# RWKV part of a hybrid layer: the distances between dependent steps set one by one, bank evictions grouped, and the mLSTM output gates computed there and passed through memory

## The chip, the cores and the metric

One core of one Trainium2 chip. The metric is the device time of one execution in microseconds (us); lower is better. TensorE is called PE here, VectorE DVE, ScalarE ACT, GpSimd POOL, and SyncE, which issues most of the loads, SP.

## The reference

One layer of a hybrid decoder on 256 positions of 2048 channels, all in float32. One wide projection `h @ w_in` feeds three mixers (a Mamba-2 scan called SSD, an RWKV-7 recurrence, an mLSTM) and three sigmoid branch gates; an output projection, a residual with LayerNorm and a gated MLP follow. Cut to what the change touches:

```python
proj = h @ w_in
(ssd_z, ssd_xbc, ssd_dt, rwkv_p, ml_qk, ml_v, ml_o, ml_i, ml_f, gate_pre) = split(proj)
# rwkv7_mixer(rwkv_p, ...), 32 heads of 64
p = p + (token_shift(p) - p) * mu
r, k, v, w_lo, a_lo, g_lo = split(p)
decay, a, g = exp(-exp(log_w)), sigmoid(a0 + a_lo @ a2), sigmoid(g_lo) @ g2
y = rwkv7_recurrence(r, decay, kh, v, -kk, kk * a)    # S_t = S_{t-1} diag(w) + (S_{t-1} a) b^T + v k^T; y = S r
y = head_layer_norm(y) * ln_w + ln_b
y = (y + sum(r * kh * r_k) * v) * g
# mlstm_mixer: 8 heads of 256 value channels
y_mlstm = sigmoid(ml_o) * (group_rms_norm(mlstm_chunked(q, k, v, ...)) * norm_w)
g_ssd, g_rwkv, g_mlstm = split(sigmoid(gate_pre))
merged = g_ssd * (y_ssd @ proj_ssd) + g_rwkv * (y_rwkv @ proj_rwkv) + g_mlstm * (y_mlstm @ proj_mlstm)
x = layer_norm(alpha * x + merged @ w_out)            # and then the gated MLP
```

## The kernel before, in words

**Weights.** Every float32 product is made of three matmuls on halves of the operands (high x high, high x low, low x high). A weight arrives in chunks of 2 x 128 rows by 512 columns: SP issues the load into `wraw` (four buffers), ACT casts the high half `whi`, DVE subtracts to get the low half `wlo` (three buffers of each), and PE multiplies. Cast and subtraction together are called a cut. One 128-row step of a projection of 512 columns is a *unit*; 16 units make a projection. In the form of r, k and v a unit is 12 matmuls of 256 columns (lines L250 to L254; output channels on partitions); in the form of the gates it is 6 matmuls of 512 columns (L272 to L274; positions on partitions). Accumulators lie in `acc` (four PSUM banks); the mixers' own matmuls use `mix` (two banks) and `seq` (two banks).

**The RWKV part** (`rwkv`) is ordered by hand on PE, DVE, ACT and POOL: in this stretch each of these engines runs its instructions in the order in which the program writes them. Two generators are interleaved. `weights()` walks the list `order` of projections: v of group 0, then for groups 1 to 3 k, v, r, one RWKV branch gate (`(1, g - 1)`) and one entry of `later` (SSD and mLSTM branch gates), and then what is left: 22 projections, 352 units. `groups()` walks the four groups of 8 heads, and a `yield n` in it says that n weight units go in before its next step. So the numbers behind `yield` are the distances, in units of PE work, between a step and the one that needs its result. If a step is not ready after that distance, PE waits.

The steps of one group, in order:
- `pre`: decay, `kh`, the normalised k.
- `pairs`: for each of four chunks, products of operands (`l1e`, `l1o`, `bk`; POOL and DVE make them), 8 matmuls into two banks (L730), four masked evictions by DVE into `bp` and into the other half of `l1e`/`l1o` (L733, L734), and transposes of `bk` with an ACT copy (L740).
- `inverse`: the triangular inverse, a chain of 31 pairs of operations on POOL (L770, L772: `si`, `yi`); beside it transposes of v and the per-head sums from `sqh` and `sql`; then a shuffle and two transposes on DVE (L791 to L795: `yi`, `x`, `xt`), and two rounds of small matmuls (L806 and after).
- `recurrence`: four chunks of dependent matmuls and evictions (`zve`, `zvo`, L853 to L867).
- `output_gate`: `gx`, `gw` by POOL, then matmuls (L896).
- `tail`: mean, squares, variance, square root, reciprocal and product on `yt` (L909 to L922), transposes of `yt` on PE (L929), an ACT activation into `yo` (L933), and two DVE products.

`weave` merges two such generators: `inverse(g)` with `tail(g - 1)`, and `recurrence(g)` with `pre(g + 1)` and `output_gate(g)`. The tail of group g thus runs while the inverse of group g+1 is under way.

In `rkv_units`, a finished projection is evicted by `lerp` (four times: an ACT activation, then a DVE part, L372 and L373), but only once the step named in `after` has been written: v of group g after `tail(g - 2)`, r after `pairs(g - 1)`, k after `kh` of g - 1. Until then the generator yields `False`: the unit is counted, and holds no matmul.

`gate_units` makes one branch gate: 16 units, a sigmoid into page `p18`, and a write to `gdram` (issued from ACT). Later `branch` reads it back.

**The rest** (SSD, branch projections, mLSTM, output projection, MLP) is ordered by a scheduler that works from the dependences. In `ml_in`, the mLSTM makes for each pair of heads a value projection, an output-gate projection (`block_tm(W, C_MO + 512 * j, ...)` and a sigmoid into `so`) and two heads (`ml_head`: scores L1076, nine value matmuls L1088, normalisation on DVE and ACT, transposes L1141, and `yml` L1148).

## Time and profile before

| | before |
|---|---|
| runs | 2484.13, 2489.2 and 2953.28 us; median 2489.2 us |
| profiled execution | 2489.84 us, span 2488.1 us |
| mean granted TensorE clock | 0.981 |
| busy | PE 2381.0 us (96%), DVE 1550.7 (62%), ACT 1244.6 (50%), POOL 447.1 (18%) |
| moved from and to memory | 443.46 MB, 178 GB/s over the span |

The profiled execution is one run under the hardware profiler; its span is what the trace covers. A "granted clock" is the share of full speed that TensorE was given. PE's busy time counts its matmuls; DVE, ACT and POOL are busy while an instruction runs. A row of waits such as "PE seq L929 <- DVE yt L922" reads: PE stood idle before an instruction of line 929 that writes `seq`, until DVE's instruction of line 922 on `yt` was done.

### The profile page before, as it was taken

How to read it: one execution, taken by the hardware profiler on the slowest of the kernel's cores; microseconds unless marked ns; L12 is line 12 of the kernel's file. 1: busy time of each engine (PE TensorE's matmuls, PEld its weight loads, DVE VectorE, ACT ScalarE, POOL GpSimd, SP SyncE). 2: the span in 40 equal slices, each digit the busy share in tenths (PEclk: the TensorE clock that was granted, in tenths of full speed). 3: DMA queues.
4: the chain of work that ended last, by engine and by line, in shares of the span. 5: the costliest groups of instructions: out<-in, count | busy, mean ns of one | idle time of the engine just before them, and what ended most of it. 6: DMA issues, size and time to landing. Idle time of an engine off the chain costs nothing.

```text
span 2488.1 us, 41458 instructions
## 1 busy us (share of the span) xinstructions
PE 2381.0 (96%) x16602; PEld 2136.5 (86%) x16602; DVE 1550.7 (62%) x1888; ACT 1244.6 (50%) x1625; POOL 447.1 (18%) x480
## 2 busy tenths in 40 slices
PE   7999989988989999999999999999999999999997
PEld 7888787787777899988899888787999999997886
DVE  6685675664664668775556666556766666664545
ACT  4635545555455546653445666444554554454333
POOL 0026333351361104330100001310300000000000
PEclk9999999999999999999999999999999999999999
DMA  8545445444455666656666667655655656557664
GB/s 236 148 138 155 126 121 155 129 138 134 145 177 164 217 178 183 191 187 231 216 188 178 183 175 219 219 188 189 183 184 182 186 179 187 184 167 231 193 196 149
DMA packets 282578, 443.46 MB, mean 178 GB/s; under 512 B 25688, under 2 KB 118288, under 8 KB 282000
## 3 DMA queue, kind: packets, MB, share of 16 engines
q1 hardware_dynamic: 279792, 431.89, 57.0%
q10 hardware_dynamic: 2016, 6.82, 0.7%
q8 instruction: 130, 2.13, 0.3%
q0 software_dynamic: 576, 2.10, 0.2%
q14 instruction: 64, 0.52, 0.1%
HBM read 428.10 MB, written 12.62 MB: 177 GB/s over the span
## 4 chain that ended last, share of the span: by engine, by line
PE 78%; POOL 5%; DVE 5%; issue 4%; ACT 4%; DMA 3%; SPq 0%; ACTq 0%; DVEq 0%; POOLq 0%
PE acc L250 13%; PE acc L254 13%; PE acc L252 13%; PE acc L272 12%; PE acc L273 11%; PE acc L274 11%; POOL yi L772 2%; POOL si L770 2%; ACT whi L157 1%; DVE wlo L158 1%; PE mix L730 1%; DVE wlo L234 1%; DMA wraw<-in_ffn_w_down 1%; PE mix L617 1%; DMA wraw<-in_proj_mlstm 1%
## 5 line engine op out<-in xcount | busy, mean ns | idle before, releaser
L234 DVE TENSOR_TENSOR wlo<-wraw,whi 128x1024 fp32r<-128x1024 f32 (+2 forms) x580 | 742.7, 1282 | 559.0 <-ACT whi L233 553.2
L233 ACT CAST whi<-wraw 128x1024 fp32r<-128x1024 f32 (+2 forms) x580 | 603.2, 1041 | 705.1 <-PE acc L274 333.2
L250 PE MATMUL acc<-xh,whi 128*128 128x256 f32 x3104 | 886.9, 286 | 6.2 <-ACT whi L233 3.8
L254 PE MATMUL acc<-xh,wlo 128*128 128x256 f32 x3104 | 882.4, 285 | 8.8 <-DVE wlo L158 6.1
L252 PE MATMUL acc<-xl,whi 128*128 128x256 f32 x3104 | 881.8, 284 | 0.0
L250 PEld LDWEIGHTS acc<-xh,whi 128*128 128x128 f32 x3104 | 598.5, 193 | 11.6 <-ACT whi L233 4.6
L254 PEld LDWEIGHTS acc<-xh,wlo 128*128 128x128 f32 x3104 | 597.9, 193 | 12.2 <-DVE wlo L158 7.6
L252 PEld LDWEIGHTS acc<-xl,whi 128*128 128x128 f32 x3104 | 598.8, 193 | 0.9 <-issue 0.7
L158 DVE TENSOR_TENSOR wlo<-wraw,whi 128x1024 fp32r<-128x1024 f32 x176 | 226.4, 1297 | 218.2 <-ACT whi L157 217.5
L272 PE MATMUL acc<-whi,xh 128*128 128x512 f32 x640 | 257.8, 415 | 5.8 <-ACT whi L157 5.8
L273 PE MATMUL acc<-wlo,xh 128*128 128x512 f32 x640 | 257.2, 402 | 4.4 <-DVE wlo L158 4.4
L274 PE MATMUL acc<-whi,xl 128*128 128x512 f32 x640 | 255.4, 399 | 0.0
L157 ACT CAST whi<-wraw 128x1024 fp32r<-128x1024 f32 x176 | 181.9, 1047 | 131.1 <-PE acc L252 74.7
L272 PEld LDWEIGHTS acc<-whi,xh 128*128 128x128 f32 x640 | 123.4, 193 | 35.7 <-ACT whi L157 6.7
L273 PEld LDWEIGHTS acc<-wlo,xh 128*128 128x128 f32 x640 | 123.7, 193 | 29.0 <-DVE wlo L158 6.6
L274 PEld LDWEIGHTS acc<-whi,xl 128*128 128x128 f32 x640 | 123.4, 193 | 26.1
L273 PE MATMUL acc<-wlo,ah 128*128 128x512 f32 x322 | 125.5, 390 | 0.7 <-DVE wlo L234 0.7
L274 PE MATMUL acc<-whi,al 128*128 128x512 f32 x322 | 125.3, 389 | 0.0
L272 PE MATMUL acc<-whi,ah 128*128 128x512 f32 x322 | 112.1, 389 | 0.8 <-ACT whi L233 0.8
L770 POOL TENSOR_TENSOR si<-yi,ni 128x126 f32<-128x126 f32 (+22 forms) x124 | 76.4, 616 | 183.6 <-DVE ni L757 174.2
L1219 POOL TENSOR_TENSOR fc<-fc 128x512 f32<-128x512 f32 (+1 forms) x22 | 27.9, 1270 | 449.7 <-DVE fc L381 444.9
L381 DVE SCALAR_TENSOR_TENSOR fc<-acc,fcols,fc 128x255 f32<-128x255 f32 (+1 forms) x172 | 77.0, 477 | 14.0 <-ACT fc L378 12.5
(357 smaller groups left out, 2993.9 us busy)
## 6 DMA issues: line engine op xcount, KB each, us to landing
wraw<-in_w_in SPq DMA_DIRECT2D x368, 512.0 KB, 3.7
wraw<-in_ffn_w_up SPq DMA_DIRECT2D x336, 256.0 KB, 3.1
wraw<-in_ffn_w_down SPq DMA_DIRECT2D x84, 512.0 KB, 4.4
wraw<-in_proj_rwkv SPq DMA_DIRECT2D x32, 512.0 KB, 4.4
wraw<-in_proj_ssd SPq DMA_DIRECT2D x32, 512.0 KB, 4.5
wraw<-in_proj_mlstm SPq DMA_DIRECT2D x32, 512.0 KB, 5.1
wraw<-in_w_out SPq DMA_DIRECT2D x32, 512.0 KB, 4.0
gdram<-gate ACTq DMA_DIRECT2D x12, 512.0 KB, 3.6
```

Source lines behind the costliest of these rows:

```text
L157: nc.scalar.copy(out=hi, in_=self.raw[i])
L158: nc.vector.tensor_tensor(out=lo, in0=self.raw[i], in1=hi.bitcast(F32), op=ALU.subtract)
L233: nc.scalar.copy(out=hi[:, :n, :width], in_=r)
L234: nc.vector.tensor_tensor(out=lo[:, :n, :width], in0=r, in1=hi[:, :n, :width].bitcast(F32), op=ALU.subtract)
L250: nc.tensor.matmul(a, lhsT=wh[:, o:o + m], rhs=X.h(kt), start=st, stop=False, skip_group_check=True)
L252: nc.tensor.matmul(a, lhsT=wh[:, o:o + m], rhs=X.l(kt), start=False, stop=False, skip_group_check=True)
L254: nc.tensor.matmul(a, lhsT=wl[:, o:o + m], rhs=X.h(kt), start=False, stop=kt == nkt - 1, skip_group_check=True)
L272: nc.tensor.matmul(acc[tt], lhsT=X.h(kt)[:, s], rhs=wh, start=kt == 0, stop=False)
L273: nc.tensor.matmul(acc[tt], lhsT=X.h(kt)[:, s], rhs=wl, start=False, stop=False)
L274: nc.tensor.matmul(acc[tt], lhsT=X.l(kt)[:, s], rhs=wh, start=False, stop=kt == nkt - 1)
L381: nc.vector.scalar_tensor_tensor(out=dst[:, j:], in0=ps[:, :T - j], scalar=v(wname, (width - 1 - j) * nch + ct), in1=dst[:, j:], op0=ALU.m ...
L770: gps.tensor_tensor(out=tv, in0=Yo[:, j:j + 1, :e].to_broadcast(sh), in1=N[:, j + 1:32, j:j + 1].to_broadcast(sh), op=ALU.mult)
```

## The change

Six edits, all in or around the RWKV part:

1. **Distances.** The numbers behind `yield` in `inverse`, `recurrence`, `output_gate` and `tail` are set anew, step by step, most of them higher; in `inverse` the pair of cast and subtraction for `sqh` and `sql` is taken apart with one unit between.
2. **Evictions of r, k and v.** All four ACT activations come first, then a `yield False`, then the four DVE parts.
3. **Pairs.** Half of the masked evictions (those into `l1e` and `l1o`) become a plain ACT copy; the mask is multiplied in three units later by POOL.
4. **Tail.** Both pairs of transposes of a bank are written before the two activations that evict it.
5. **Output gates of the mLSTM.** They join `later` as four more projections of the RWKV part (26 projections, 416 units) and go to `gdram`, whose first axis grows from 3 to 4. `ml_in` no longer computes them; it reads `so` back by a DMA on SP.
6. With that, two entries of `later` follow each group's gate instead of one.

```diff
...
 COL = {"r": C_R, "k": C_K, "v": C_V}
+def gate_column(i, j):
+    return 512 * j + (C_GATE + 2048 * i if i < 3 else C_MO)
...
         for j in range(4):
-            self.lerp(cts[j], t[:, j], self.v("mu_" + nm, 4 * g + j),
-                      self.omm[:, 16 * i + 4 * g + j:16 * i + 4 * g + j + 1])
+            self.nc.scalar.activation(out=t[:, j], in_=cts[j], func=AF.Identity,
+                                      scale=self.omm[:, 16 * i + 4 * g + j:16 * i + 4 * g + j + 1])
+        yield False
+        for j in range(4):
+            self.nc.vector.scalar_tensor_tensor(out=t[:, j, 1:], in0=cts[j][:, :T - 1],
+                                                scalar=self.v("mu_" + nm, 4 * g + j), in1=t[:, j, 1:],
+                                                op0=ALU.mult, op1=ALU.add)
         self.t[nm, g] = t
...
-        later = [(i, j) for i in (0, 2) for j in range(NB)]
+        later = [(i, j) for i in (0, 2, 3) for j in range(NB)]
         order = [("v", 0)]
         for g in range(1, 4):
-            order += [("k", g), ("v", g), ("r", g), (1, g - 1), later.pop(0)]
+            order += [("k", g), ("v", g), ("r", g), (1, g - 1), later.pop(0), later.pop(0)]
         order += [(1, 3)] + later
-        col = lambda a, b: C_GATE + 2048 * a + 512 * b if a in (0, 1, 2) else COL[a] + 512 * b
+        col = lambda a, b: COL[a] + 512 * b if a in COL else gate_column(a, b)
         self.ahead = Ahead(self, [(W, [(0, col(a, b), 512)]) for a, b in order])
...
                 vec.tensor_tensor(out=uc(BP)[H[e], c], in0=ps[H[e]], in1=mg[H[e]].to_broadcast([64, 4, P]), op=ALU.mult)
-                vec.tensor_tensor(out=uc(L1[e])[H[1 - e], c], in0=ps[H[1 - e]],
-                                  in1=mg[H[1 - e]].to_broadcast([64, 4, P]), op=ALU.mult)
+                nc.scalar.copy(out=uc(L1[e])[H[1 - e], c], in_=ps[H[1 - e]])
             yield 3
+            for e in range(2):
+                lk = uc(L1[e])[H[1 - e], c]
+                gps.tensor_tensor(out=lk, in0=lk, in1=mge[e][H[1 - e]].to_broadcast([64, 4, P]), op=ALU.mult)
             ps = self.bank("seq").rearrange("p (c t) -> p c t", c=4)
...
             gps.tensor_tensor(out=Yo[:, j + 1:32, :e], in0=Yo[:, j + 1:32, :e], in1=tv, op=ALU.subtract)
+        yield 1
...
                 nc.scalar.copy(out=ZV[1][H[0], :, 2 * tt + cc], in_=ps[H[cc], :, 64:128])
+            yield 1
         sqh, sql = self.p4(8, "sqh", F32R), self.p4(9, "sql", F32R)
-        self.split(sqh, sql, sq)
-        yield 4
+        nc.scalar.copy(out=sqh, in_=sq)
+        yield 1
+        vec.tensor_tensor(out=sql, in0=sq, in1=sqh.bitcast(F32), op=ALU.subtract)
+        yield 3
         for b in range(2):
...
             vec.tensor_tensor(out=v[:, 2 * b:2 * b + 2], in0=v[:, 2 * b:2 * b + 2], in1=ps, op=ALU.mult)
-        yield 22
+        yield 24
         vec.stream_shuffle(out=Yc[:, :, :, 1], in_=Yo, mask=[i % 16 + 16 for i in range(32)])
...
         vec.transpose(out=XT.rearrange("p u t -> p t u")[:, 0:32], in_=Y)
-        yield 3
+        yield 4
         for q in (1, 3):
...
                 nc.scalar.copy(out=ZV[e][H[e], :, c], in_=RU[H[e], 1])
-            yield 2
+            yield 3
             if c < 3:
...
                 nc.scalar.copy(out=yt[H[c % 2], c // 2, :, e], in_=Yc[H[1 - e]])
-            yield 2
+            yield 3
         self.g_[g] += (yt,)
...
         self.split(gx[:, 0], gx[:, 1], self.glo, nc.gpsimd)
-        yield 1
-        yield 1
+        yield 4
         gg = self.p4(16, "gg")
...
         vec.tensor_tensor(out=yv, in0=yv, in1=sm.unsqueeze(2).to_broadcast([P, 16, 64]), op=ALU.subtract)
-        yield 2
+        yield 3
         y2 = self.pg("p14", [P, 16, 64], "y2")
         nc.scalar.activation(out=y2, in_=yv, func=AF.Square)
-        yield 1
+        yield 2
         sv = self.cp.tile([P, 16], F32, name="hsm", bufs=2)
         vec.tensor_reduce(out=sv, in_=y2, axis=AX.X, op=ALU.add)
-        yield 1
+        yield 2
         nc.scalar.activation(out=sv, in_=sv, func=AF.Sqrt, scale=1.0 / 64, bias=self.c("eps", 1, 1))
-        yield 1
+        yield 2
         vec.reciprocal(out=sv, in_=sv)
         vec.tensor_tensor(out=yv, in0=yv, in1=sv.unsqueeze(2).to_broadcast([P, 16, 64]), op=ALU.mult)
-        yield 2
+        yield 4
         yo = self.p4(14, "yo")
...
                                         identity=self.c("ident"))
+            for j in range(2):
                 ct = 2 * b + j
...
             yield 1
+        yield 1
         vec.tensor_tensor(out=yo, in0=yo, in1=v, op=ALU.add)
...
                            acc[tt].rearrange("p (h v) -> p h v", h=2))
-            acc = self.block_tm(W, C_MO + 512 * j, self.X)
             so = self.pg("p%d" % (10 + j), [P, 2, 512], "mso")
-            for tt in range(2):
-                nc.scalar.activation(out=so[:, tt], in_=acc[tt], func=AF.Sigmoid)
+            nc.sync.dma_start(out=so, in_=self.gdram[:, 3, j])
             self.vt.append(vt)
...
     def gate_units(self, i, j):
-        acc = yield from self.tm_units(self.a["w_in"], C_GATE + 2048 * i + 512 * j, self.X)
+        acc = yield from self.tm_units(self.a["w_in"], gate_column(i, j), self.X)
         g = self.pg("p18", [P, 2, 512], "gate")
...
         self.ydram = self.dp.tile([P, KT, T], F32, name="ydram")
-        self.gdram = self.dp.tile([P, 3, 4, 2, 512], F32, name="gdram")
+        self.gdram = self.dp.tile([P, 4, 4, 2, 512], F32, name="gdram")
         self.L1 = [self.pg("b0", [P, 16, P], "l1e"), self.pg("b1", [P, 16, P], "l1o")]
...
```

Line numbers of the changed program are higher by 6 to 18 in these functions. Three places show how the instructions move.

On DVE, the place is the tail of group 0, which runs beside the inverse of group 1. `y_...` holds the squares, `hsm` the per-head sums, `yt` the output of the recurrence, `yo` that of the tail, and `wlo` is a weight cut. Before:

```order
L917 TENSOR_REDUCE hsm<-y_3809 128x16
L789 TENSOR_TENSOR v<-v,mix 128x512 x2
L921 RECIPROCAL hsm<-hsm 128x16
L922 TENSOR_TENSOR yt<-yt,hsm 128x1024
L936 TENSOR_TENSOR yo<-yo,v 128x1024
L937 TENSOR_TENSOR yo<-yo,gg 128x1024
L373 SCALAR_TENSOR_TENSOR v<-acc,cst,v 128x255 x4
L158 TENSOR_TENSOR wlo<-wraw,whi 128x1024 x8
```

The same place on DVE in the changed program:

```order
L933 TENSOR_REDUCE hsm<-y_3896 128x16
L164 TENSOR_TENSOR wlo<-wraw,whi 128x1024
L806 TENSOR_TENSOR v<-v,mix 128x512 x2
L164 TENSOR_TENSOR wlo<-wraw,whi 128x1024
L937 RECIPROCAL hsm<-hsm 128x16
L938 TENSOR_TENSOR yt<-yt,hsm 128x1024
L954 TENSOR_TENSOR yo<-yo,v 128x1024
L955 TENSOR_TENSOR yo<-yo,gg 128x1024
L553 SCALAR_TENSOR_TENSOR v<-acc,cst,v 128x255 x4
L164 TENSOR_TENSOR wlo<-wraw,whi 128x1024 x7
```

Two cuts have moved in between the sum of squares and the reciprocal; between the product on `yt` and the two on `yo` there is no cut in either program, and the eviction of v stands right behind.

On POOL, the place is the last chunk of `pairs` of group 0 and the start of the inverse behind it (`nk`, `pext`, `av` and `cs` are operands from `pre`; `cst` holds the masks). Before:

```order
L713 TENSOR_TENSOR l1e<-nk,pext 64x4x64
L715 TENSOR_TENSOR bk<-av,cs 64x4x64
L713 TENSOR_TENSOR l1o<-nk,pext 64x4x64
L715 TENSOR_TENSOR bk<-av,cs 64x4x64
L763 MEMSET yi 128x1024
L765 COPY yi<-cst 128x16 x2
```

The products of operands run straight into the start of the inverse. In the changed program:

```order
L724 TENSOR_TENSOR l1e<-nk,pext 64x4x64
L726 TENSOR_TENSOR bk<-av,cs 64x4x64
L724 TENSOR_TENSOR l1o<-nk,pext 64x4x64
L726 TENSOR_TENSOR bk<-av,cs 64x4x64
L749 TENSOR_TENSOR l1e<-l1e,cst 64x4x128
L749 TENSOR_TENSOR l1o<-l1o,cst 64x4x128
L749 TENSOR_TENSOR l1e<-l1e,cst 64x4x128
L749 TENSOR_TENSOR l1o<-l1o,cst 64x4x128
L776 MEMSET yi 128x1024
L778 COPY yi<-cst 128x16 x2
```

Four products with the mask (those of the third and of the fourth chunk) now stand between the last operands and the start of the inverse.

On PE, the place lies between heads 5 and 6 of the mLSTM; L1076 and L1077 (L1092 and L1093 in the changed program) are the scores of head 6, L1141 (L1158) the transposes of head 5, and L272 to L274 are large matmuls of a projection. Before:

```order
L272 MATMUL acc<-whi,xh 128x512 x2
L1076 MATMUL mix<-mqk 128x256
L1077 MATMUL mix<-mqk 128x128
L273 MATMUL acc<-wlo,xh 128x512
L274 MATMUL acc<-whi,xl 128x512
L1141 MATMUL mix<-cst,mn 128x128 x3
L273 MATMUL acc<-wlo,xh 128x512
L274 MATMUL acc<-whi,xl 128x512
```

In this program 56 large matmuls stand between the last value matmuls of head 5 and the first of head 6. In the changed program the place reads (L278 to L280 are the large matmuls, here of the mLSTM branch projection):

```order
L1104 MATMUL mix<-mvt,mes 128x258 x6
L280 MATMUL acc<-whi,yml 128x512 x2
L1158 MATMUL mix<-cst,mn 128x128
L1092 MATMUL mix<-mqk 128x256
L1093 MATMUL mix<-mqk 128x128
L1158 MATMUL mix<-cst,mn 128x128 x3
L1104 MATMUL mix<-mvt,mes 128x258 x2
L278 MATMUL acc<-whi,ymh 128x512
L279 MATMUL acc<-wlo,ymh 128x512
L278 MATMUL acc<-whi,ymh 128x512
L279 MATMUL acc<-wlo,ymh 128x512
L1104 MATMUL mix<-mvt,mes 128x258
```

There, two large matmuls stand between the last value matmuls of head 5 and the first of head 6.

## The prediction

> **What bounds the kernel now.** First the page: TensorE's share of the span and the chain that ended last.
>
> ```profile
> span 2488.1 us, 41458 instructions
> PE 2381.0 (96%) x16602; PEld 2136.5 (86%) x16602; DVE 1550.7 (62%) x1888; ACT 1244.6 (50%) x1625; POOL 447.1 (18%) x480
> PE 78%; POOL 5%; DVE 5%; issue 4%; ACT 4%; DMA 3%; SPq 0%; ACTq 0%; DVEq 0%; POOLq 0%
> ```
>
> PE carries the kernel; what a re-timing can win is what the chain holds of POOL, DVE, ACT and issue. Where that lies, the busy times by stretch tell: the start and the bulk of the RWKV part, and the eight mLSTM heads. Columns: stretch, its length, busy time and count of PE, weight loads, DVE, ACT and POOL, the granted TensorE clock, DMA share, GB/s.
>
> ```profile
> 90.00:150.00 60.00, 50.79 (x347) 45.62 (x346) 42.87 (x62) 28.65 (x43) 19.75 (x21) 0.87 0.41 122
> 150.00:840.00 690.00, 634.93 (x5219) 543.23 (x5220) 421.20 (x492) 354.07 (x516) 245.84 (x355) 0.95 0.50 147
> ...
> 1350.00:1571.00 221.00, 220.47 (x1035) 183.29 (x1034) 143.73 (x224) 138.58 (x210) 11.35 (x8) 1.00 0.66 197
> ```
>
> The RWKV stretch is the leaky one: from 150 to 840 PE idles 690.0 - 634.9 = 55.1 us, and its clock is 0.95, so another 0.05 x 690 = 34.5 us goes to half speed. From 90 to 150 it is 9.2 + 7.8 = 17.0 us. The mLSTM heads (1350 to 1571) leak 0.5 us: there PE is full.
>
> What PE waited for between 90 and 840 (total us, times, longest):
>
> ```profile
> PE seq L929 <- DVE yt L922: 18.5, 4, 7.9
> PE seq L839 <- DVE zve L867: 7.2, 4, 2.5
> PE acc L254 <- DVE wlo L158: 6.1, 7, 1.3
> PE acc L272 <- ACT whi L157: 5.8, 2, 3.2
> PE seq L929 <- ACT yo L933: 5.2, 7, 1.0
> PE acc L273 <- DVE wlo L158: 4.4, 5, 1.4
> PE seq L859 <- ACT zvo L853: 2.4, 2, 1.2
> PE mix L788 <- DVE sql L291: 2.4, 3, 1.0
> PE mix L896 <- POOL gx L291: 2.1, 3, 0.8
> PE seq L806 <- DVE x L793: 2.0, 1, 2.0
> ```
>
> Each is a dependent step for which too few weight units were put between. Of DVE and ACT neither is full (61% and 51% of that stretch): these are latencies, not throughput.
>
> **The change, part by part.** A unit is one 128-row step of a projection. Its price comes from starts of neighbouring matmuls:
>
> ```profile
> 571.86 0.39 PE L272 MATMUL acc<-whi,xh 128*128 128x512 f32 x1
> 572.08 0.39 PE L273 MATMUL acc<-wlo,xh 128*128 128x512 f32 x1
> ...
> 355.43 0.28 PE L788 MATMUL mix<-sqh,ones 128*128 128x256 f32 x1
> 355.55 0.28 PE L788 MATMUL mix<-sql,ones 128*128 128x256 f32 x1
> 363.68 0.69 PE L929 MATMUL seq<-cst,yt 128*128 128x128 f32 x2 [7.86 <-DVE yt L922]
> ```
>
> 512 columns take 0.227 us, 256 take 0.12: a gate unit (6 x 512) is 1.36 us, an r, k or v unit (12 x 256) 1.44 us. The four output gates bring 4 x 16 = 64 units, 87 us, from the mLSTM stage into RWKV; on PE this is a move at no price. They pay for the longer distances: following the generators, the dependent steps use 350 of 352 units now, 406 of 416 then.
>
> *Tails (18.5 + 5.2 us).* From the mean to the transposes there were 3, 6, 7 and 7 units for the four groups; now 9, 12, 13 and 13. The first had 3 because v of group 2 may not be evicted before tail 0 is done (`after`): the stream then yields without work, and the 7.86 us row above is the price. That rule stays, so tail 0 keeps a wait. Its square root now comes two units ahead; left are the reciprocal and the 1.24 us multiply, behind one weight cut: 1.5 us, and about 2 us for cuts that stand behind `yo`. The other three waited 10.6 us together, 3.5 each, behind 6 or 7 units (9 to 10 us): a chain of some 13 us, which now gets 12 x 1.4 = 17, so nothing waits. The two transposes per bank now precede both activations: the 5.2 us go. Left: 3.5 of 23.7.
>
> *Inverse (2.0 + 5.8 us, and part of the 4.4).* Here POOL is the rival clock:
>
> ```profile
> 339.15 1.09 PE mix L730 x16
> ...
> 393.20 1.32 DVE yi L791 x2
> 394.54 2.23 DVE x L793
> 396.77 1.86 DVE xt L795
> ```
>
> From the last pair's matmuls to the first inverse result on DVE are 54 us, to `x` 57.6 us, whatever PE does. Units from those matmuls to L806 were 36, 30, 33, 36 and become 40, 33, 39, 42, at 1.4 us, with an estimated 4 us of pair, sum and transpose matmuls between: 60, 50, 59, 63 us. Only group 1 (8 units lost to tail 0) stays short, by some 2 us beside its tail's waits; and DVE, held 5.5 us by the shuffle and two transposes, then delays one cut by about 3. Groups 1 and 2 lost 5.8 us at L272 (above) because ACT stood in the middle of the eviction of r, waiting 6.0 us for DVE:
>
> ```profile
> 398.93 0.84 ACT L372 ACTIVATE r<-acc,omm 128x256 f32<-128x256 f32 x2 [6.03 <-DVE r L373]
> ```
>
> With the four activations ahead of the four DVE parts that wait cannot hold casts. Left: 6 of 12.
>
> *Recurrence and output gate (7.2 + 0.5 + 2.4 + 2.1 us).* Two of three distances go from 2 to 3 units (+1.4 us each), the gate's from 2 to 4. Waits of up to 1.4 vanish, the 2.5 us one keeps 1.1: left 2. *sql* (2.4): left 0.
>
> *Pairs.* 32 DVE evictions go, 32 ACT copies and 32 POOL products come:
>
> ```profile
> L734 DVE TENSOR_TENSOR l1e<-mix,cst x16: 694/694/695, 152.2 to 684.7; 64x512 f32<-64x512 f32 x16
> L740 ACT COPY bk<-seq x16: 583/588/589, 155.8 to 688.8; 128x512 f32<-128x512 f32 x16
> L715 POOL TENSOR_TENSOR bk<-av,cs x32: 724/741/1717, 133.9 to 651.2; 64x256 f32<-64x256 f32 x32
> ```
>
> DVE gains 22 us, ACT pays 32 x 0.59 = 19, POOL 32 x 1.48 = 47 (twice the 256-element row). POOL then has 4 x 0.74 + 2 x 1.48 = 5.9 us per chunk of some 9 (the pitch of the pairs), and the product's first reader is the recurrence, over 35 units later: nothing on the path. If the products delayed the inverse by their last pair, it would be 4 x 3 = 12 us; behind the bank's release, nothing. I take 0.
>
> Ten evictions (r, k, v) use a unit without matmuls; that is in the counts. The four more gate writes are ACT issues between casts; the four reads stand on SP among the last `proj_rwkv` loads, with up to seven chunks of two units (2.7 us) fetched or cut ahead. I take 0; a late load would cost one landing, 4 us.
>
> Idle left in 150 to 840: 3.5 + 6 + 2 + 4 of other cuts + 1.5 small = 17 of 55. The clock: half speed follows waits of this length:
>
> ```profile
> 619.00:622.00 3.00, 0.53 (x4) 0.19 (x2) 2.90 (x5) 1.15 (x2) 0.00 (x0) 1.00 0.63 176
> 622.00:627.00 5.00, 4.95 (x42) 3.62 (x43) 2.24 (x3) 1.34 (x3) 0.86 (x1) 0.66 0.36 103
> ```
>
> A wait of 2.5 us was followed by 0.66 over 5 us, 1.7 us lost. With 17 of 55 idle left I keep 11 of 34.5. The stretch before 150 stays. **Gain 55 + 34.5 - 28 = 62 us** (bounds: everything, 90; or half, 45).
>
> The Trainium skill (TensorE: Matmul & The Clock Gate, "Why this matters for your kernels") says that only PE gaps above about 3 us bring half clock back. This row speaks against it, with 2.5 us. By the rule, hardly a wait that I expect to remain would cost clock, and the sum would come out 11 us lower, at 2431.
>
> *mLSTM (a loss).* Without the output gates the heads lose their filler. The scheduler's new order leaves, from the first value matmul of head 4 to the last transposes of head 7, only 21 units: 46, 8, 24 and 48 large matmuls for heads 4 to 7. What a head takes by itself:
>
> ```profile
> 1555.33 0.41 PE L1088 MATMUL mix<-mvt,mes 128*128 128x258 f32 x2
> ...
> 1568.61 1.23 DVE L234 TENSOR_TENSOR wlo<-wraw,whi 128x1024 fp32r<-128x1024 f32 x1 [1.64 <-ACT whi L233]
> 1570.77 0.48 DVE L1148 SCALAR_TENSOR_TENSOR yml<-mix,cst,ymh 128x256 fp32r<-128x256 f32 x1 [0.54 <-ACT ymh L1147]
> ```
>
> Head 7 took 15.9 us from its first value matmul to the end of `yml`, with five weight cuts in its way (the last is shown): 15.9 at most, about 11 if each cost it 1 us. PE has, at 0.227 us a matmul plus some 1.9 us of the head's own (nine value matmuls at 0.12, scores and transposes), 12, 4, 7 and 13 us for heads 4 to 7. At 11 PE waits 0 + 7 + 4 + 0 = 11 us; at 15.9, 4 + 12 + 9 + 3 = 28. I take 11, the cuts being few there, plus 3 us of clock: **loss 14 us** (0 to 31).
>
> **Sum.** The profiled execution took 2489.84 us (span 2488.1), level with the median 2489.2. 2489.8 - 62 + 14 = **2442 us**, 1.9% less. About 2% (50 us) is what a measurement of this kernel tells from no change, so the forecast lies just inside.
>
> **Rivals.**
> 1. *Nearly all waits go*: 15 us are left in the stretch, with hardly any half clock behind such short waits: 75 us won, heads lose 8: 2423. For it: DVE and ACT are half idle there. Against: tail 0 keeps its rule.
> 2. *POOL takes the place of the distances*: inverse waits in three groups (6 us with clock each) and half the recurrence's waits stay: 45 us won, heads lose 22: 2467. For it: 54 us fixed against my 59 to 63 in groups 0 and 2.
> 3. *The products on POOL hold the cuts.* The trace has a DVE product of 0.42 us (median) stretched while POOL multiplies:
>
> ```profile
> 460.29 2.18 DVE L867 TENSOR_TENSOR zve<-zm,pl 64x256 f32<-64x256 f32 x1
> 462.15 1.48 POOL L291 TENSOR_TENSOR gx<-glo__767,gx 128x512 fp32r<-128x512 f32 x1
> ...
> L157 ACT CAST whi<-wraw 128x1024 fp32r<-128x1024 f32 x176 | 181.9, 1047 | 131.1 <-PE acc L252 74.7
> ```
>
> If each of the 32 products put its 1.48 us on a cut that PE needs, 47 us would go: 2489. The slack speaks against it: after PE frees a buffer, two chunks (5.5 us) remain while a cut needs 1.05 us on ACT and 1.23 on DVE. I give it a tenth; half the price, 2466. The Trainium skill (SBUF — State Buffer, "Who interferes with whom") states the rule: a DVE instruction with two SBUF inputs and a GpSimd instruction that reads SBUF exclude each other. This trace agrees, with 2.18 against 0.42 us.
> 4. *Heads set the pace* (slower). Their pitch, by the score matmuls of heads 1, 2 and 3:
>
> ```profile
> 1402.65 0.60 PE L1076 MATMUL mix<-mqk 128*128 128x256 f32 x2
> 1422.24 0.59 PE L1076 MATMUL mix<-mqk 128*128 128x256 f32 x2
> 1451.13 0.59 PE L1076 MATMUL mix<-mqk 128*128 128x256 f32 x2
> ```
>
> 19.6 and 28.9 us. PE work over eight heads falls to about 105 us (66 units, 8 x 1.9), 13.1 a head. At 28.9 for each the loss is 231 - 105 = 126, and the time 2489.8 - 62 + 126 = 2554. It turns slower above (105 + 62) / 8 = 21 us. Against: the long pitch held 17 units of work and the wait for the gate.
>
> **Chances.** Forecast (2432 to 2452) 0.42; rival 1 0.27; rival 2 0.18; rival 3 0.10; rival 4 0.03. The range runs from rival 1 with its bound (90 won, heads lose 8: 2408) to the other bounds met at once (45 won, heads lose 31: 2476). Faster by over 2% (below 2439.4): rival 1 and some two fifths of the forecast, 0.44. Slower by over 2%: 0.03. Within: 0.53.
>
> **What would show it.** The RWKV stretch is 87 us longer in work and 62 shorter in waits, some 775 us instead of 750: the tail's transposes wait for `yt` once, under 4 us; none waits for `yo` or `gx`; the clock is 0.97 to 0.98; ACT without a 6 us wait in the r eviction. The mLSTM stretch takes some 150 us instead of 221, with PE waiting at the transposes of heads 5 and 6. I am wrong if waits for POOL's result stand in three groups, if weight cuts on DVE run far above 1.23 us, or if head pitches stay above 15 us to the end.

## The result: 2450.9 us against 2489.2 us, 1.5% less

| | before | after |
|---|---|---|
| median of the runs | 2489.2 us (2484.13 to 2491.26; one more run than above) | 2450.88 us (2449.08 to 2452.13) |
| ratio | 1 | 0.9849, 95% interval 0.9829 to 0.987 |
| span of the profiled execution | 2488.1 us | 2450.1 us |

The one run of 2953 us of before is left out of the median and of the ratio as disturbed. The span fell by 38.0 us. Measured at the same points in both traces (the last matmul of the RWKV part's projections, the first scores of the mLSTM, the last matmul on `ymh`), the RWKV part ends at 868.8 us instead of 830.4: 38.4 us later with 87.2 us more work, so it won 48.8. SSD and branches take 525 us in both. The stretch of the heads and their projection takes 208.7 instead of 285.7, 77.0 less with 87.2 less work: it lost 10.2. The rest is level.

First the parts of the page of after that answer to those of before:

```profile
span 2450.1 us, 41499 instructions
PE 2369.3 (97%) x16602; PEld 2131.2 (87%) x16602; DVE 1546.7 (63%) x1856; ACT 1247.3 (51%) x1648; POOL 509.5 (21%) x512
PE 83%; POOL 6%; DVE 4%; ACT 3%; DMA 2%; issue 2%; SPq 0%; DVEq 0%; ACTq 0%; POOLq 0%
```

POOL's share of the chain rose while DVE's and ACT's fell. Busy times by stretch (columns as before): the two RWKV stretches and the heads.

```profile
90.00:150.00 60.00, 53.58 (x382) 49.27 (x382) 41.65 (x65) 30.86 (x48) 12.44 (x12) 0.89 0.44 135
150.00:868.00 718.00, 692.21 (x5472) 592.81 (x5472) 453.90 (x482) 394.63 (x576) 318.10 (x395) 0.97 0.55 164
1393.60:1602.30 208.70, 198.05 (x914) 163.24 (x913) 134.86 (x221) 118.25 (x187) 31.81 (x18) 0.98 0.61 189
```

In the bulk PE now idles 718.0 - 692.2 = 25.8 us, where it was 55; the clock is 0.97 instead of 0.95. What it still waits for between 90 and 920:

```profile
PE acc L279 <- DVE wlo L164: 9.8, 4, 4.8
PE seq L823 <- DVE x L810: 5.7, 1, 5.7
PE acc L260 <- DVE wlo L164: 4.5, 5, 1.2
PE mix L528 <- DVE s_gs L514: 1.8, 1, 1.8
PE mix L805 <- DVE sql L799: 1.8, 1, 1.8
PE acc L256 <- ACT whi L163: 1.7, 1, 1.7
PE seq L945 <- DVE yt L938: 1.7, 1, 1.7
...
```

The rows left out are of 1.6 us and less.

The rows for `zve`, `zvo`, `yo` and `gx` are gone, that for `yt` fell from 18.5 to 1.7. In their place stand late cuts (L279) and `x` (L823). Both have one cause, which the view of one line, POOL's last operation of the inverse, tells (who waited for it: us, times), before and then after:

```profile
  DVE yi L791: 4.5, 2
```

```profile
  DVE yi L808: 17.1, 4
```

DVE waits at the shuffle for POOL's chain, now in all four groups. The weight cuts are queued behind it. Group 3, on DVE and on PE:

```profile
745.74 1.23 DVE L164 TENSOR_TENSOR wlo<-wraw,whi 128x1024 fp32r<-128x1024 f32 x1 [1.50 <-ACT whi L163]
751.60 0.01 DVE L808 LOAD_MASK_SELECT yi<-yi  x1 [4.63 <-POOL yi L785]
751.60 1.30 DVE L808 STREAM_SHUFFLE yi<-yi 128x512 f32<-128x512 f32 x1
752.94 2.00 DVE L810 STREAM_TRANSPOSE x<-yi 128x1024 f32<-128x1024 f32 x1
754.84 1.85 DVE L812 STREAM_TRANSPOSE xt<-yi 128x1024 f32<-128x1024 f32 x1
756.56 2.31 DVE L164 TENSOR_TENSOR wlo<-wraw,whi 128x1024 fp32r<-128x1024 f32 x2
```

```profile
757.81 0.79 PE L279 MATMUL acc<-wlo,xh 128*128 128x512 f32 x1 [4.80 <-DVE wlo L164]
```

For 9.6 us (746.97 to 756.56) DVE works on no cut, PE runs dry for 4.8 us, and half clock follows (behind the shuffles of groups 0, 1 and 3):

```profile
232.00:240.00 8.00, 8.00 (x78) 6.22 (x79) 2.21 (x2) 3.14 (x5) 1.24 (x4) 0.50 0.62 199
402.00:411.00 9.00, 6.23 (x74) 4.91 (x75) 8.04 (x10) 4.48 (x6) 1.87 (x5) 0.50 0.35 118
757.00:766.00 9.00, 8.19 (x78) 6.41 (x79) 3.10 (x3) 5.20 (x8) 1.66 (x4) 0.50 0.71 227
```

The half clock lasts until 241.1, 411.7 and 766.7 us. From the end of each wait (231.9, 404.7 and 757.8 us) that makes 9.1, 7.0 and 8.9 us at half speed, so 4.6, 3.5 and 4.5 us of clock on top of the waits of 3.3, 5.7 and 4.8 us.

### The profile page after: what moved, and what is told of

Same layout as the page of the kernel before. It is cut to its first block, busy times and chain, and to the rows that moved or that the text cites. A ratio compares the mean times of both kernels' runs of the same rounds, so it can differ in the third digit from the quotient of the medians.

```text
span 2450.1 us, 41499 instructions
## 1 busy us (share of the span) xinstructions
PE 2369.3 (97%) x16602; PEld 2131.2 (87%) x16602; DVE 1546.7 (63%) x1856; ACT 1247.3 (51%) x1648; POOL 509.5 (21%) x512
## 4 chain that ended last, share of the span: by engine, by line
PE 83%; POOL 6%; DVE 4%; ACT 3%; DMA 2%; issue 2%; SPq 0%; DVEq 0%; ACTq 0%; POOLq 0%
PE acc L256 13%; PE acc L260 13%; PE acc L258 13%; PE acc L278 13%; PE acc L279 12%; PE acc L280 12%; POOL yi L785 3%; POOL si L783 2%; POOL res L360 1%; DVE wlo L164 1%; PE mix L741 1%; ACT whi L163 1%; DVE wlo L240 1%; PE mix L628 1%; PE mix L1023 1%
## 5 line engine op out<-in xcount | busy, mean ns | idle before, releaser
L240 DVE TENSOR_TENSOR wlo<-wraw,whi 128x1024 fp32r<-128x1024 f32 (+2 forms) x548 | 703.3, 1284 | 519.5 <-ACT whi L239 514.2
L239 ACT CAST whi<-wraw 128x1024 fp32r<-128x1024 f32 (+2 forms) x548 | 569.6, 1041 | 656.5 <-PE acc L280 298.9
L256 PE MATMUL acc<-xh,whi 128*128 128x256 f32 x3104 | 885.1, 286 | 4.9 <-ACT whi L239 2.9
L256 PEld LDWEIGHTS acc<-xh,whi 128*128 128x128 f32 x3104 | 597.3, 193 | 9.2 <-ACT whi L239 3.5
L164 DVE TENSOR_TENSOR wlo<-wraw,whi 128x1024 fp32r<-128x1024 f32 x208 | 278.6, 1351 | 239.1 <-ACT whi L163 238.9
L163 ACT CAST whi<-wraw 128x1024 fp32r<-128x1024 f32 x208 | 216.7, 1049 | 118.3 <-PE acc L280 58.3
L279 PE MATMUL acc<-wlo,xh 128*128 128x512 f32 x640 | 255.5, 399 | 9.9 <-DVE wlo L164 9.8
L278 PE MATMUL acc<-whi,xh 128*128 128x512 f32 x640 | 262.1, 414 | 0.1
L280 PE MATMUL acc<-whi,xl 128*128 128x512 f32 x640 | 253.9, 397 | 0.0
L279 PEld LDWEIGHTS acc<-wlo,xh 128*128 128x128 f32 x640 | 122.9, 192 | 34.5 <-DVE wlo L164 12.0
L278 PEld LDWEIGHTS acc<-whi,xh 128*128 128x128 f32 x640 | 122.4, 191 | 29.5 <-issue 1.2
L280 PEld LDWEIGHTS acc<-whi,xl 128*128 128x128 f32 x640 | 122.9, 192 | 26.3
L279 PE MATMUL acc<-wlo,ah 128*128 128x512 f32 x322 | 125.4, 389 | 0.2 <-DVE wlo L240 0.2
L280 PE MATMUL acc<-whi,al 128*128 128x512 f32 x322 | 125.3, 389 | 0.0
L278 PE MATMUL acc<-whi,ah 128*128 128x512 f32 x322 | 111.9, 389 | 0.0
L785 POOL TENSOR_TENSOR yi<-yi,si 128x126 f32<-128x126 f32 (+22 forms) x124 | 84.9, 684 | 9.7
```

The lines of the kernel that those rows point to most:

```text
L163: nc.scalar.copy(out=hi, in_=self.raw[i])
L164: nc.vector.tensor_tensor(out=lo, in0=self.raw[i], in1=hi.bitcast(F32), op=ALU.subtract)
L239: nc.scalar.copy(out=hi[:, :n, :width], in_=r)
L240: nc.vector.tensor_tensor(out=lo[:, :n, :width], in0=r, in1=hi[:, :n, :width].bitcast(F32), op=ALU.subtract)
L256: nc.tensor.matmul(a, lhsT=wh[:, o:o + m], rhs=X.h(kt), start=st, stop=False, skip_group_check=True)
L278: nc.tensor.matmul(acc[tt], lhsT=X.h(kt)[:, s], rhs=wh, start=kt == 0, stop=False)
```

## Experiments 1: where the gain comes from

Medians, with the ratio to the kernel before on the same chip in each case. The runs were made on different chips, so two of them are compared by their ratios where a few us matter. Four kernels take the change apart into the moved output gates (edit 5), the second gate per group (edit 6) and the local edits (1 to 4).

**The kernel before with edits 5 and 6 alone**; distances and evictions stay.

```diff
-        later = [(i, j) for i in (0, 2) for j in range(NB)]
+        later = [(i, j) for i in (0, 2, 3) for j in range(NB)]
...
-            order += [("k", g), ("v", g), ("r", g), (1, g - 1), later.pop(0)]
+            order += [("k", g), ("v", g), ("r", g), (1, g - 1), later.pop(0), later.pop(0)]
...
+            nc.sync.dma_start(out=so, in_=self.gdram[:, 3, j])
```

> The kernel before with the output gates alone moved (old distances, old evictions, two gates per group). Theory A: every wait of before stays in the RWKV part, 87 us of work change place, and the heads lose their 10 us: 2500 us, slower than before by 0.4%. Rival (the move itself wins, since its units fill what was empty): under 2470 us.

Measured: 2479.27 us, 0.9957 (0.9939 to 0.9975). It lies between the two forecasts: it won 9 us. The RWKV part alone won 19.9 (it ends at 897.7 us: 67.3 later with 87.2 more work).

**The changed kernel without edits 5 and 6.**

```diff
-        later = [(i, j) for i in (0, 2, 3) for j in range(NB)]
+        later = [(i, j) for i in (0, 2) for j in range(NB)]
...
-            order += [("k", g), ("v", g), ("r", g), (1, g - 1), later.pop(0), later.pop(0)]
+            order += [("k", g), ("v", g), ("r", g), (1, g - 1), later.pop(0)]
...
-            nc.sync.dma_start(out=so, in_=self.gdram[:, 3, j])
+            acc = self.block_tm(W, C_MO + 512 * j, self.X)   # and the sigmoid into so
```

> The changed kernel without the output gates: they are computed in the mLSTM part again, so the RWKV part has 352 units for distances that ask for 406. Theory A (the units of the output gates pay for the distances): 54 units of 1.4 us are missing, 76 us of uncovered steps, in the inverses of groups 1 and 2 and at the end (recurrence and tail of group 3), with some 10 us of clock; the heads win their 10 us back: 2451 + 76 + 10 - 10 = some 2525 us, slower than before. Rival (the distances and the regrouping win by themselves, the move only costs the heads): 2441 us.

Measured: 2463.18 us, 0.9899 (0.9884 to 0.9914). This is where my theory fell. With 54 units too few the kernel is not slower than before, it has two thirds of the gain. Counted from the generators, 24 of the 54 are missing past the last unit and 30 are empty units more in the middle. PE waits in the middle (12.4 us for `x`, 7.6 for `sqh`), and behind the last unit it waits for nothing. These two results gave theory B: it is the second gate per group, not the output gates, that supplies the middle groups. Two kernels test it.

**The kernel before with the second gate per group, and nothing else.**

```diff
-            order += [("k", g), ("v", g), ("r", g), (1, g - 1), later.pop(0)]
+            order += [("k", g), ("v", g), ("r", g), (1, g - 1), later.pop(0), later.pop(0)]
```

> The kernel before with one word of its order changed: two gates of later per group instead of one (nothing moved from the mLSTM part, all distances as before). Between the last pair and the shuffle stand 31, 31, 31, 31 units instead of 31, 25, 28, 31, and the tail of group 0 has 7 instead of 3 before its transposes. Theory B (the second gate per group is half of the change's gain; the moved output gates are no part of it): as the kernel with the gates alone moved, without its loss at the heads: 2479 - 11 = 2468 us. Rival (the units of the output gates are needed): 2479 us or more.

Measured: 2463.93 us, 0.9898 (0.9883 to 0.9913). One word of the order is worth 25 of the change's 38 us. Why is seen by counting units: with one gate per group the stream runs out of work that it may finish (v of group 2 waits for tail 0, r for the pairs) and yields empty units. Between the last pair and the shuffle of groups 1 and 2 there were 25 and 28 units, with the second gate 31 and 31, and tail 0 had 7 instead of 3.

**The changed kernel with edit 6, without edit 5.**

```diff
-        later = [(i, j) for i in (0, 2, 3) for j in range(NB)]
+        later = [(i, j) for i in (0, 2) for j in range(NB)]
...
-            nc.sync.dma_start(out=so, in_=self.gdram[:, 3, j])
+            acc = self.block_tm(W, C_MO + 512 * j, self.X)   # and the sigmoid into so
```

> The changed kernel with its order (two gates of later per group), but the output gates stay in the mLSTM part: later holds 8 entries, so the RWKV part has 352 units and none is left for the last recurrence and tail. Theory B (formed after the first runs: the units matter in groups 1 and 2, where the second gate per group supplies them; at the end the scheduler puts matmuls of the SSD part between, so missing units cost nothing): the waits of the changed kernel, and the heads keep their filler: 2451 - 10 = 2441 us. Rival (the 54 missing units are missed at the end): 2460 us or more.

Measured: 2438.28 us, 0.9806 (0.9791 to 0.9821): 11 us less than the changed kernel by the ratios (12.6 by the medians), and the intervals lie apart. The move of the output gates is a loss. Up to the shuffle of group 3 its units stand as in the changed kernel; all 54 are missing behind it, and PE waits only some 6 us there. Its RWKV and SSD parts together end at 1305.9 us; those of after at 1393.6, less 87.2 of work 1306.4: the same. And the heads keep their filler. PE's waits in the stretch of the heads, of after, then of this kernel:

```profile
PE mix L1158 <- DVE mn L1116: 5.0, 1, 5.0
PE mix L1158 <- POOL merged L1146: 3.1, 1, 3.1
PE mix L1092 <- DVE mn L1111: 0.8, 1, 0.8
...
```

```profile
PE mix L1160 <- POOL merged L1148: 3.4, 1, 3.4
PE mix L1160 <- DVE mn L1118: 0.6, 1, 0.6
```

What fills the end is seen on PE in the timeline of this kernel: the last matmul of the last gate unit, then the SSD part's projection (L256), and much later the RWKV part's own steps.

```profile
751.74 0.39 PE L280 MATMUL acc<-whi,xl 128*128 128x512 f32 x1
751.96 0.28 PE L256 MATMUL acc<-xh,whi 128*128 128x256 f32 x1
...
768.50 0.28 PE L256 MATMUL acc<-xh,whi 128*128 128x256 f32 x1
770.41 0.27 PE L862 MATMUL seq<-zve,l1e 128*64 128x64 f32 x1 [1.63 <-ACT xt L836]
...
831.33 1.04 PE L945 MATMUL seq<-cst,yt 128*128 128x128 f32 x8
```

The hand-written order holds among the instructions of the RWKV part; the scheduler puts those of the next part between them where PE would wait.

By the ratios (before 1, with the second gate 0.9898, with the local edits too 0.9806, with the moved gates too 0.9849) the second gate is worth 25 us and the local edits 23, and the moved output gates cost 11. That these three add up to the whole is no test, since each is taken from where the last one ended. The test is the other order: the local edits without the second gate win 25 us (0.9899), and the moved gates cost 15 us in the kernel that has the second gate and no local edit (0.9957 against 0.9898). So each part is worth about as much with the others as without.

## Experiments 2: the local edits one by one

**The tail as before** in the changed kernel: its five distances, and transposes and activations alternating.

```diff
-        yield 3    # and 2, 2, 2, 4, and 1 more behind the activations
+        yield 2    # and 1, 1, 1, 2
...
-            for j in range(2):
                 ct = 2 * b + j
```

> The changed kernel with the tail as before (distances, and transposes and activations alternating). By the working of the forecast the waits for yt and yo come back, 12 to 18 and 5 us, with some 7 us of clock: 2470 us. Rival (the longer tail 0 takes 6 units from the inverse of group 1, since v of group 2 waits for it; with the old tail that inverse has 34 units again, and its wait of 5.7 us and 5 us of clock go): 2458 us.

Measured: 2463.35 us, 0.9907 (0.9892 to 0.9922), 12 us more than after. The waits for `yt` (6.6) and `yo` (5.4) are back, but the inverse of group 1 got its 6 units back and PE no longer waits for `x`: both readings hold a part, and the tail is worth about 12 to 14 us.

**The evictions of r, k and v as before**: ACT and DVE alternating, no empty unit.

```diff
-        yield False
...
+            self.lerp(cts[j], t[:, j], self.v("mu_" + nm, 4 * g + j), ...)
```

> The changed kernel with the evictions of r, k and v as before (each ACT activation followed by its DVE part, no empty unit between). By the working of the forecast the casts are held again where ACT waits for DVE in the middle of the eviction of r: 5.8 us, and 2 to 5 us of clock: 2457 to 2461 us. Rival (those waits came from the place of the eviction, behind the inverse's transposes on DVE, which the second gate per group has moved; the kernel with the second gate alone waits 2.1 us for such casts): 2451 us.

Measured: 2457.7 us, 0.9882 (0.9866 to 0.9899): 7 to 8 us more than after, as the forecast had it, though the two intervals just overlap, so the size is not sure. PE waits again 4.7 us for casts (five times, 1.8 at most), and 4.0 at tail 0, beside an inverse that has three units fewer here.

**The recurrence and the output gate at their old distances.**

```diff
-            yield 3    # twice per chunk
+            yield 2
...
-        yield 4
+        yield 1
+        yield 1
```

> The changed kernel with the distances of the recurrence (2 instead of 3 units) and of the output gate (1 + 1 instead of 4) as before. By the working of the forecast the waits for zve, zvo and gx come back, 7.2 + 2.4 + 2.1 less 2 us, with a few us of clock: 2451 + 10 to 15 = 2461 to 2466 us. Rival (these waits were short, and 25 units fewer are asked for, so other steps gain): 2451 us.

Measured: 2454.91 us, 0.9864 (0.9847 to 0.988). Against after that is not clear of the intervals, and far from 10 to 15 us. The short waits came back:

```profile
PE acc L279 <- DVE wlo L164: 16.8, 7, 5.8
PE acc L260 <- DVE wlo L164: 10.2, 6, 5.4
PE mix L913 <- POOL gx L297: 3.4, 4, 1.3
PE seq L856 <- DVE zve L884: 2.9, 3, 1.3
...
PE seq L867 <- ACT rsb L859: 1.3, 1, 1.3
```

The three rows of short waits are 7.6 us together, and no half clock followed them. The freed units give the inverse of group 1 six units more, and the wait for `x` is gone; but the rows for late cuts (the first two) grew from 14.3 to 27.0 us. What the distances are worth by themselves is not shown.

**The pairs' masks on DVE again**, no product on POOL.

```diff
-                nc.scalar.copy(out=uc(L1[e])[H[1 - e], c], in_=ps[H[1 - e]])
+                vec.tensor_tensor(out=uc(L1[e])[H[1 - e], c], in0=ps[H[1 - e]], in1=mg[H[1 - e]]..., op=ALU.mult)
```

> The changed kernel with the masked evictions of the pairs on DVE again: no products on POOL. Theory A (POOL's products are done 5 us before the inverse's first operand is there and cost nothing): from the last pair's matmuls to the shuffle stays 55 to 58.5 us, and the time 2451 +- 5 us. Rival (POOL's chain grew from 41-43 to 42-46 us because of the products): 53 to 57 us again, the three waits behind the shuffle each 2 us shorter: 2440 us.

Measured: 2449.83 us, 0.9845 (0.983 to 0.9859): the same. From the last pair's matmuls to the shuffle it took 54.2, 55.2, 57.9 and 58.5 us, against 55.2, 56.5, 57.9 and 58.5 in after. The products cost nothing, and no gain of edit 3 can be seen.

## Experiments 3: what paces it now, and a faster version

**A gate between k and v**, so that v of group 2 isn't held by tail 0.

```diff
-            order += [("k", g), ("v", g), ("r", g), (1, g - 1), later.pop(0), later.pop(0)]
+            order += [("k", g), later.pop(0), ("v", g), ("r", g), (1, g - 1), later.pop(0)]
```

> The changed kernel with one line of the order changed: a gate stands between k and v of each group, so that v of group 2 is finished after tail 0 and the stream doesn't yield empty units. Between the last pair and the shuffle of group 1 stand 35 units instead of 28, in the others 35, 34 and 36. Theory A (the inverse of group 1 is short because of the rule that v of group 2 waits for tail 0): the wait of 5.7 us before the matmuls on x, its 5 us of half clock and the 1.7 us before the tail's transposes go: 2439 us. Rival (POOL's chain of 56 us is late there whatever PE does, or v now comes late for the next pairs): 2449 us or more.

Measured: 2449.62 us, 0.9843 (0.9828 to 0.9858): nothing won. The waits for `x` and `yt` are gone, as theory A said, and the cuts are late instead, once behind each of the four shuffles:

```profile
PE acc L260 <- DVE wlo L164: 17.8, 7, 6.0
PE acc L279 <- DVE wlo L164: 8.8, 8, 5.8
...
```

PE had more units before the shuffle and POOL's chain in group 1 became 3 us longer (59.5 us from the last pair); it was POOL that set the end, whatever stood before it.

**That order, and more units before the shuffle.**

```diff
-        yield 24
+        yield 28
```

> The changed kernel with a gate between k and v and with 28 instead of 24 units before the shuffle: 39, 39, 39 and 40 units between the last pair's matmuls and the shuffle, where it had 34, 28, 34 and 36. Theory C (POOL's chain of 55 to 59 us paces the inverse; DVE waits for it at the shuffle, and the cuts behind that are late): the three waits of 3.3, 5.7 and 4.8 us go, and with them three times 5.1 us of half clock: 2426 us. Rival (the chain on POOL grows with what runs beside it, so the shuffle stays late): 2445 us.

Measured: 2444.62 us, 0.9829 (0.9813 to 0.9845). The waits behind the shuffles shrank (PE's idle time from the last pair to 12 us behind the shuffle fell from 3.3, 8.5, 1.8 and 4.8 us in after to 0, 1.4, 1.1 and 3.1), but from there to the first matmul of the next pairs it grew from 0.8, 1.5 and 1.6 us to 5.4, 4.8 and 3.3. DVE shows it:

```profile
281.39 0.87 DVE L686 SCALAR_TENSOR_TENSOR nk<-k,cst,mix 128x256 f32<-128x256 f32 x2
282.29 3.39 DVE L692 TENSOR_TENSOR av<-av,nk 128x1024 f32<-128x1024 f32 x1
285.61 1.28 DVE L694 COPY pl<-pext 128x16 f32<-128x16 f32 x1
286.80 3.61 DVE L702 SCALAR_TENSOR_TENSOR sq<-r,cst,kh 128x256 f32<-128x256 f32 x4
290.33 3.32 DVE L164 TENSOR_TENSOR wlo<-wraw,whi 128x1024 fp32r<-128x1024 f32 x2
```

No cut is made for 9 us, and PE waits 5.0 us. The distance between these steps is one unit here as in the changed kernel; but there a cut fell among them in two of the three groups (between L694 and L702, at 454.13 and 629.31 us), and with the gate between k and v none does.

**That order and distance without edit 5** (`later` without index 3, the output gates in `ml_in`).

> The two kernels above in one: later_shuffle with the output gates in the mLSTM part. Theories B and C together: 2426 - 10 = 2416 us. Rival (the inverse of group 3 has 22 units of its own and the SSD part doesn't fill the rest): 2440 us.

Measured: 2446.85 us, 0.984 (0.9824 to 0.9856). The rival: the inverse of group 3 has 22 units of its own, and PE waits 11.5 us for `x` there. The SSD part fills a recurrence, but not that long inverse.

**Two output gates moved instead of four, the gate between k and v, 27 units before the shuffle, and two longer distances in `pre`.**

```diff
-        later = [(i, j) for i in (0, 2, 3) for j in range(NB)]
+        later = [(i, j) for i in (0, 2) for j in range(NB)] + [(3, 0), (3, 1)]
...
         self.split(nrr[:, 0], nrr[:, 1], nr)
-        yield 2
+        yield 3
...
         vec.tensor_copy(out=PL, in_=pe[:, :, 64])
-        yield 1
+        yield 3
...
-        yield 24
+        yield 27
```

> The changed kernel with two of the four output gates in the mLSTM part again (those of heads 4 to 7), a gate between k and v, 27 units before the shuffle instead of 24, and two distances in the preparation of the next group longer (3 instead of 2 units before the matmuls on nrr, 3 instead of 1 before the products with r). Theory B and C: the heads 4 to 7 have their filler (-8 us), the shuffle has 38, 38, 38, 39 units, and the cluster of DVE work in the preparation, 8 us without a cut, which took the gain of the longer shuffle distance, is parted: 2451 - 8 - 20 = 2423 us. Rival (POOL's chain grows again): 2440 us.

Measured: 2416.6 us, 0.9712 (0.9696 to 0.9729): 2.9% less than before, and 34 us less than the change. Its stretches, and what PE waits for:

```profile
90.00:150.00 60.00, 53.20 (x394) 49.44 (x393) 42.74 (x68) 30.76 (x47) 12.60 (x12) 0.91 0.44 140
150.00:790.00 640.00, 625.23 (x5047) 538.10 (x5047) 415.65 (x452) 361.67 (x527) 308.55 (x387) 1.00 0.53 165
```

```profile
PE acc L279 <- DVE wlo L164: 6.6, 5, 3.3
PE mix L684 <- DVE nk L686: 5.4, 3, 2.8
PE acc L260 <- DVE wlo L164: 4.5, 4, 2.0
...
```

14.8 us of idle in the bulk, and full clock. How much each of its four edits brings was not taken apart.

## Why the prediction was right, and where its steps failed

The time lay 9 us above the forecast and inside the range; the forecast was within 2%, and so it came. The RWKV part won 49 us where 62 were forecast, and the heads lost 10 where 14 were: 13 too much on one side and 4 too much on the other make the 9. The stretch of 778 us (90 to 868; 775 forecast) agrees by luck: the forecast's 750 us ran to 840, and the projections of before ended at 830, so to the same point it should have been 765. From the first score to the last `yml` it took 148 us (150 forecast). The parts of the sum were not all what they were taken for.

- **"They pay for the longer distances"** is the step that failed. The units of the output gates pay for nothing: without them the time is 11 to 13 us lower. I took the shortage (406 units used, 352 without these) as if PE would be empty past the last unit, and the scheduler fills that place. What the distances of groups 1 and 2 needed was the second gate per group, which I had only in the counts of units (12, 13 and 33, 39) and not as a cause. The total survived since those counts were right for the changed kernel, whichever edit brought them; that the forecast gave the credit to the wrong edit did not show in it.
- **Tails**: 3.5 us forecast to be left, 1.7 measured; `yo` gone, as told.
- **Inverse**: this step failed too, by a sign that the prediction had named itself: waits for POOL's result stand on DVE in all four groups, and PE runs dry behind them in three. I took 57.6 us from the last pair's matmuls to `x` as fixed, from group 1 alone, and found only group 1 short. Measured from the last of these matmuls to the end of the transpose into `x`, it was 56.8, 56.8, 59.1 and 60.5 us before and 58.7, 59.9, 61.5 and 61.8 after; POOL's chain alone took 41.0, 41.6, 43.1 and 43.5 us before and 42.9, 43.8, 46.3 and 47.0 after. Why it grew is not shown. And I compared the time to `x` with PE's arrival at the matmuls on `x` alone. PE came there 64, 54, 63 and 67 us after the pairs, later than `x` in three groups; in groups 0 and 3 it ran dry ahead of that point, on the cuts that stand behind DVE's shuffle. That is the first half of rival 2, and dearer than it said: 3.3 + 5.7 + 4.8 us of waits and 12.6 us of clock, 26 us for three groups instead of 3 x 6. Its other half, waits in the recurrence, did not come.
- **Clock**: 11 us forecast to be left in the bulk, 0.026 x 718 = 19 measured, most of it behind those waits. With 26 us of idle time left there instead of 17, this makes the RWKV part some 17 us worse than forecast; the stretch before 150, which the forecast left as it was, won 4 of them back (6.4 us idle and 6.6 of clock, instead of 9.2 and 7.8). So the RWKV part won 49 and not 62.
- **Recurrence, output gate**: waits of 2 us forecast, no row of theirs left; but the kernel without these distances came out only 4 us slower, not 10 to 15, and by its interval that is not told from nothing.
- **Evictions of r, k, v**: about 6 forecast, 7 to 8 measured. **Pairs**: 0 forecast, 0 measured; the product took 1.09 us, not 1.48. Rival 3 is out. (In its rows, the POOL product that ran beside the 2.18 us was the one before the one shown, on `gw`, from 459.31 to 462.2.)
- **Heads**: 14 us of loss forecast, 10 to 13 measured. PE waits at the transposes of head 5 (5.0 us) as told, not at head 6; the heads' pitch fell to 9.7 us at the end, so rival 4 never came near. Against rival 1 stand the 26 us of idle time in the bulk, where it had 15.

## What to carry over

Where work is interleaved by hand, first look whether the stream that fills the gaps is ever held empty by its own rules: here one more job per round in the order gave as much as resetting a dozen distances. Filler taken from a later stage has to be paid for there, and past the end of a hand-ordered stretch a scheduler may find filler by itself, so try the new order without the move. When short waits are gone, a long chain on another engine comes next, and it is felt through what is queued behind the engine that waits for it (here cuts behind a shuffle), so it needs units of its own.

## What the chip showed that I had not expected

Half clock follows shorter waits than those I had priced, and not all of them. In after, waits of 1.78 us (at 537.56) and 1.22 us (at 622.51) were each followed by it, and one of 1.65 us (at 370.83) by none:

```profile
537.56 0.38 PE L805 MATMUL mix<-sql,ones 128*128 128x256 f32 x1 [1.78 <-DVE sql L799]
622.51 0.38 PE L684 MATMUL mix<-nrr,ones 32*128 32x256 f32 x1 [1.22 <-DVE nk L686]
```

```profile
371.00:378.00 7.00, 6.94 (x58) 6.73 (x57) 4.35 (x7) 5.05 (x10) 6.22 (x11) 1.00 0.24 81
538.00:542.00 4.00, 4.00 (x23) 4.00 (x22) 4.00 (x5) 1.36 (x2) 3.61 (x6) 0.57 0.73 240
623.00:627.00 4.00, 4.00 (x12) 3.15 (x12) 3.87 (x6) 1.11 (x2) 2.84 (x2) 0.57 0.48 131
```

0.43 x 4 = 1.7 us lost each time. The rule of the Trainium skill that the prediction weighed (TensorE: Matmul & The Clock Gate, "Why this matters for your kernels": gaps above about 3 us) does not hold in these rows. But the length of a wait alone does not decide either. In the kernel with edit 6 and without edit 5, the same 1.22 us before the same line (L684, ending at 623.08) were followed by full clock, and so was the wait of 3.3 us before L279 (ending at 763.16) in the fastest kernel:

```profile
623.00:630.00 7.00, 6.92 (x57) 5.47 (x58) 6.87 (x10) 3.01 (x5) 5.27 (x4) 1.00 0.28 77
763.00:770.00 7.00, 6.84 (x88) 5.58 (x89) 3.04 (x4) 3.60 (x5) 1.48 (x4) 1.00 0.69 225
```

So no price that goes by the length of the wait alone, as the prediction's did, fits all of these rows. What decides was not tried.
